# Decay and beta columns taken along by the spatial gate's value projection

## The chip, the cores and the metric

One core of a Trainium2 chip runs the whole program. Its engines work side by side, each through its own list of instructions: TensorE (PE; its weight loads are listed as PEld), VectorE (DVE), ScalarE (ACT), GpSimd (POOL) and SyncE (SP), from whose queue almost all transfers are issued. The metric is device time in microseconds (us) of one execution; lower is better.

## The reference

Two layers of a block whose mixer has four branches of 256 features: a retention, a spatial gate, a short convolution and a gated delta rule. There are 1024 latent and 256 context tokens of 1024 features; all is float32. Per layer, cut to what this change concerns:

```python
h  = rms_norm(x, g_pre[l]) * (1.0 + scale[:, None]) + shift[:, None]       # the same for ctx
p  = h @ w_in[l]                       # 15 pieces of 256 columns, then 4 of 4: a_f, a_b, b_f, b_b
# spatial gate: u, v, z are pieces 4, 5, 6
v = layer_norm_plain(gelu(v));  s = einsum('hij,bnjhd->bnihd', w_s, v) + b_s
y = gelu(u) * s * silu(z)
# gated delta rule: for both directions, chunks of 64 tokens, 4 heads
g    = -exp(a_log) * softplus(a + dt_bias);   beta = sigmoid(b)
gc   = cumsum of g within a chunk;            g_last = its last value
decay = exp(gc_i - gc_j);  k_tail = kc * exp(g_last - gc);  c_dec = exp(g_last)
```

The 16 last columns of `p` give the decays `a` and the betas `b` of 2 directions and 4 heads. The second layer computes outputs for the latent tokens alone, but its keys, values, decays and betas also for the context.

## The kernel before

**Number format.** TensorE multiplies float32 with several passes; the kernel writes both operands of its large products as a high and a low float32r part and adds three products (high x high, high x low, low x high). `halve` makes the parts: ACT casts the high one, POOL (or DVE) subtracts the low one. `H` holds the parts of h, feature-major in three token blocks of 512, 512 and 256.

**Projections.** `projs` (lines 511 to 513) is feature-major: 128 columns of weights are stationary, tokens move, 512 at a time, eight pieces of features one after the other. `proj_tm` (lines 534 to 536) is token-major: 128 tokens of h are stationary and 256 columns of weights move, so a tile of tokens has 24 passes. It serves the values of the spatial gate and of the retention. Both write to one of two PSUM banks of pool `pj`. Weights come through the tags `raw`, `whi` and `wlo`, two buffers each.

**Decays and betas.** They have a product of their own in plain float32: `gate_part` (line 409) multiplies each of the eight pieces of h with 32 columns (16 of them zero) into the bank `pb`, four pieces side by side; `gate_rows` copies `pb` to SBUF on ACT (line 414) and adds the four with a matrix of ones (line 419) into `ab`: rows 32 g + (direction, head), 320 tokens a row. In layer 0 that is done as h is made (`first_h`), in layer 1 within the output stage of layer 0 (`make_h_gates`). `gates` (lines 867 to 918) then makes softplus, betas and the running sums by two scans over the rows, all on [128, 320] tiles on DVE and ACT, stores them to DRAM (`gc`, `last`) and turns them to token-major columns `vtok` by 40 matmuls with selecting matrices (lines 912, 913).

**Order of a layer.** `run` first drains `delta_qkv(l, ctx, 0)`: keys and values of the first pair of heads, then queries; `gates` stands in it behind keys and values. Then for each pair `delta_chain`: triangles, their inverse (`lanes`, `invert`) and 20 steps in a row, three small products each (lines 1107, 1116, 1130) with DVE work between; and `delta_out` (line 1171). What TensorE does in the meantime comes from `fillers`, a generator over short convolution, spatial gate, the second pair's projections (`qkv`), the first pair's gate (`fin0`), and the retention (`rv`, `r0`, `r1`), the other half of the convolution (`sc1`) and `fin1`. `beside(pe, wait)` pulls as much of it as the waits ahead are planned to last; `fin0` gives nothing until the first pair's outputs are there:

```python
self.lead = min(self.lead, 4.0) + pe - wait * 1.4
least = 0.6 * pe
while self.lead < 0 or least > 0:
    us = next(self.flow, None)
```

**The scheduler.** The framework orders each engine's instructions at build time: what is written earlier goes first, and what is written later moves up where an earlier instruction is not ready, as far as tiles can be had. Most tiles are slots of 1280 floats: 10 in pool G, 7 in pool F. In the start-up, loads are chained in order by `inorder`; `ahead` holds the three steps that make h, popped as a projection reaches a token block.

Of the kernel before, what the change touches and what calls it, by code (L numbers as in the profile page):

```python
# [19 lines left out]
P = 128  # L20
D = 1024
KC = 8
# [12 lines left out]
# columns of the constant array  # L35
C_ID = 0
C_SUM = C_ID + 128
C_MASK = C_SUM + 32
# [5 lines left out]
C_ROW = C_INDQ + 32  # L44
C_SELA = C_ROW + 6
C_SELD = C_SELA + 4 * 24
C_PM = C_SELD + 4 * 24
C_PH = C_PM + 2
C_N = C_PH + 2


def constants():
    """Tables that depend on shapes alone."""
# [3 lines left out]
    c[:, C_SUM:C_SUM + 32] = np.tile(np.eye(32), (4, 1))  # L57
# [17 lines left out]
    c[:, C_ROW + 0] = np.where(r < 8, 1.0, np.where(r < 16, -1.0, 0.0))  # L75
    c[:, C_ROW + 1] = np.where(r < 16, -1.0, 0.0)
    c[:, C_ROW + 2] = r < 4
    c[:, C_ROW + 3] = (r >= 4) & (r < 8)
    c[:, C_ROW + 4] = (r >= 8) & (r < 16)
    for g in range(4):  # L80
        for k in range(8):
            a, b = 32 * g + k, 32 * g + 8 + k
            o = C_SELA + g * 24
            c[a, o + k] = 1.0
            c[b, o + 8 + k] = 1.0
            c[b, o + 16 + k] = 1.0
            c[a, C_SELD + g * 24 + 8 + k] = 1.0
    c[:, C_PM] = np.where(r < 16, -1.0, 0.0)
    c[:, C_PM + 1] = np.where(r >= 16, -1.0, 0.0)
    c[:, C_PH:C_PH + 2] = -c[:, C_PM:C_PM + 2]  # L90
    return c


def rotary():
    """cos and signed sin of the grid positions, [d of two heads, (cos | sin), token]."""
# [9 lines left out]
class Block:  # L105
    """The two layers, on one core."""
# [23 lines left out]
    # ---------------------------------------------------------------- tiles  # L130
# [16 lines left out]
    def small(self, shape, nm, bufs=None):  # L147
        self.uid += 1
        k = {} if bufs is None else {"bufs": bufs}
        tag = nm if nm in ("hf", "hg", "wab0", "wab1", "xn") else f"{nm}{self.layer}"  # L150
# [12 lines left out]
    # ---------------------------------------------------------------- set-up  # L163
    def setup(self):
# [33 lines left out]
    def features(self):  # L198
        """Per-feature vectors as columns: the steps that load them, and the one that turns them."""
# [79 lines left out]
    def gate(self, l):  # L279
        """gate * g_post as rows, to DRAM: the steps that make them."""  # L280
# [25 lines left out]
    # ---------------------------------------------------------------- h  # L306
# [5 lines left out]
    def rstd(self, out, ss):  # L312
        """(mean + eps) ** -0.5 of sums over the features"""
# [13 lines left out]
    def first_h(self):  # L327
        """h of the first layer, from the inputs."""
# [40 lines left out]
        def block(b, t0, n):  # L369
# [8 lines left out]
            pb = self.ps("pb")  # L378
            hs = []
            for kc in range(KC):  # L380
# [10 lines left out]
                hs.append(hf)  # L391
                if kc % 4 == 3:
                    for j in range(kc - 3, kc + 1):
                        self.gate_part(pb[:, :n], j, hs[j])
            self.gate_rows(pb, t0, n)

        self.gate_weights(0)
# [3 lines left out]
    def gate_weights(self, l):  # L401
        self.wab = self.small([P, KC, 32], f"wab{l}", 1)
        self.nc.gpsimd.memset(self.wab, 0.0)
        self.inorder(self.nc.sync.dma_start(self.wab[:, :, :16], self.wcols(l, 15 * 256, 16)))
        self.pab = self.ps("ab")

    def gate_part(self, out, kc, h):
        r = 32 * (kc % 4)
        return self.nc.tensor.matmul(out[r:r + 32], lhsT=self.wab[:, kc], rhs=h, start=(kc < 4), stop=(kc >= 4))  # L409

    def gate_rows(self, pb, t0, n):
        """Their sums: rows 32 g + (direction, head), 320 tokens of group g."""
        part = self.small([P, 512], "hg", 1)
        self.nc.scalar.copy(part[:, :n], pb[:, :n])
        t = t0
        while t < t0 + n:
            g, o = t // 320, t % 320
            m = min(320 - o, t0 + n - t)
# [1068 lines left out]
```

## Time and profile before

| | us |
|---|---|
| median of 3 runs (lowest to highest) | 1568.75 (1561.75 to 3282.81) |
| span of the profiled execution | 1566.5 |
| PE busy in it | 1464.3 (93%) |
| DVE, ACT, POOL busy | 815.3, 491.6, 389.0 |

The profile is of one execution, from its first to its last instruction; the median of the runs is 2.25 us above its span. Times in the views count from the span's start. Layer 0 goes to about 872 us (from 738 with its output stage), layer 1 from there on. A busy PE includes the tail of a matmul that the next one overlaps. PE's idle time is mostly in the start-up, in the two inversions of the second pairs and behind the last chain.

### The profile page before, as it was taken

What the parts mean: (1) busy time and instruction counts of PE and PEld (TensorE: products, weight loads), DVE (VectorE), ACT (ScalarE), POOL (GpSimd) and SP (SyncE); (2) the same over time, 40 slices, a digit from 0 to 9 for tenths busy, and PEclk for the clock granted to TensorE, in tenths of its full rate; (3) what the DMA queues carried; (4) which work ended last, traced back from release to release, by engine and by line L of the source; (5) the groups of instructions that cost most, each with busy time, mean ns of one, the idle gap of its engine ahead of it and who ended that gap; (6) DMA issues with size and microseconds to landing.
All of it is one profiled execution on the core that took longest, in us unless ns stands there. A gap on an engine that the chain in (4) does not pass through costs nothing.

```text
span 1566.5 us, 35585 instructions
## 1 busy us (share of the span) xinstructions
PE 1464.3 (93%) x14962; PEld 1133.4 (72%) x14962; DVE 815.3 (52%) x1851; ACT 491.6 (31%) x1053; POOL 389.0 (25%) x567
## 2 busy tenths in 40 slices
PE   4899999999998889999999999999999869999698
PEld 1377887666786666778899787866678557666698
DVE  0656753453277566454355566534543876554333
ACT  3534223212331222324455451322222312322331
POOL 2322222231131113223212132222321312133221
PEclk9899999999999899999999999999999898999899
DMA  8412430235565211036433235322125341113552
GB/s 274 150 28 67 120 68 23 65 126 171 156 157 130 51 50 42 26 116 188 155 122 123 67 78 133 85 69 83 61 72 132 86 102 44 28 55 106 173 193 81
DMA packets 210250, 158.91 MB, mean 101 GB/s; under 512 B 95142, under 2 KB 182442, under 8 KB 210090
## 3 DMA queue, kind: packets, MB, share of 16 engines
q1 hardware_dynamic: 209578, 156.63, 35.8%
q8 instruction: 117, 1.92, 0.5%
q14 instruction: 43, 0.35, 0.1%
q0 software_dynamic: 512, 0.00, 0.0%
HBM read 123.84 MB, written 32.76 MB: 100 GB/s over the span
## 4 chain that ended last, share of the span: by engine, by line
PE 75%; DVE 11%; issue 6%; DMA 4%; ACT 2%; SPq 1%; POOL 1%; DVEq 0%; POOLq 0%; ACTq 0%
PE pj L511 14%; PE pj L513 13%; PE pj L512 12%; PE po L1383 4%; PE po L1381 4%; PE po L1382 4%; PE cb L1116 3%; DVE lt L1227 2%; PE pb L409 2%; PE cb L1130 2%; PE cb L1107 2%; DMA wm<-in_w_mod 1%; DVE xl L1229 1%; POOL wlo L472 1%; PE pt L535 1%
## 5 line engine op out<-in xcount | busy, mean ns | idle before, releaser
L472 POOL TENSOR_TENSOR wlo<-raw,whi 128x512 fp32r<-128x512 f32 x152 | 208.4, 1384 | 593.9 <-ACT whi L471 547.4
L1381 PE MATMUL po<-wo,whi 128*128 128x256 f32 x576 | 163.1, 284 | 1.3 <-ACT wo L471 1.3
L1383 PE MATMUL po<-wo,wlo 128*128 128x256 f32 x576 | 162.7, 282 | 1.2 <-POOL wlo L472 1.2
L1382 PE MATMUL po<-wo,whi 128*128 128x256 f32 x576 | 161.8, 281 | 0.3 <-DVE wo L472 0.3
L1139 POOL COPY gS<-cS 64x64 f32<-64x64 f32 x304 | 86.2, 284 | 284.8 <-DVE cS L1136 261.5
L471 ACT CAST whi<-raw 128x512 fp32r<-128x512 f32 x152 | 92.1, 618 | 179.3 <-PE pj L512 95.4
L1381 PEld LDWEIGHTS po<-wo,whi 128*128 128x128 f32 x576 | 108.8, 189 | 4.4 <-issue 2.4
L1383 PEld LDWEIGHTS po<-wo,wlo 128*128 128x128 f32 x576 | 109.0, 189 | 3.1 <-POOL wlo L472 1.8
L1382 PEld LDWEIGHTS po<-wo,whi 128*128 128x128 f32 x576 | 109.1, 189 | 0.9 <-DVE wo L472 0.5
L1110 DVE SCALAR_TENSOR_TENSOR cy<-cb,vtok,gvt 64x64 f32<-64x64 f32 x304 | 73.8, 280 | 67.5 <-PE cb L1107 66.0
L1124 ACT COPY gx<-cb 64x128 f32<-64x128 f32 x160 | 41.6, 260 | 213.7 <-DVE cw L1121 200.1
L511 PE MATMUL pj<-h10h,whi 128*128 128x512 f32 x200 | 86.7, 434 | 1.8 <-ACT rk L738 1.8
L511 PE MATMUL pj<-h00h,whi 128*128 128x512 f32 x200 | 84.8, 425 | 2.0 <-ACT h00h L385 2.0
L511 PE MATMUL pj<-h11h,whi 128*128 128x512 f32 x200 | 85.2, 426 | 0.0
L511 PE MATMUL pj<-h01h,whi 128*128 128x512 f32 x200 | 83.6, 418 | 0.9 <-ACT gp L928 0.9
L513 PE MATMUL pj<-h00h,wlo 128*128 128x512 f32 x200 | 82.8, 414 | 0.9 <-POOL wlo L472 0.9
L513 PE MATMUL pj<-h10h,wlo 128*128 128x512 f32 x200 | 82.6, 413 | 0.4 <-POOL wlo L472 0.4
L512 PE MATMUL pj<-h10l,whi 128*128 128x512 f32 x200 | 82.4, 412 | 0.0
L512 PE MATMUL pj<-h00l,whi 128*128 128x512 f32 x200 | 82.3, 412 | 0.0
L512 PE MATMUL pj<-h11l,whi 128*128 128x512 f32 x200 | 81.7, 408 | 0.0
L1121 DVE TENSOR_TENSOR cw<-cb,gwt 64x128 f32<-64x128 f32 x152 | 43.9, 289 | 72.6 <-PE cb L1116 70.6
L513 PE MATMUL pj<-h11h,wlo 128*128 128x512 f32 x200 | 80.8, 404 | 0.0
(375 smaller groups left out, 3448.2 us busy)
## 6 DMA issues: line engine op xcount, KB each, us to landing
raw<-in_w_in SPq DMA_DIRECT2D x120, 256.0 KB
wm<-in_w_mod SPq DMA_DIRECT2D x32, 512.0 KB
x<-in_x SPq DMA_DIRECT2D x16, 512.0 KB
wg<-in_w_mod SPq DMA_DIRECT2D x16, 512.0 KB
raw<-yd SPq DMA_DIRECT2D x32, 256.0 KB
gD<-gc SPq DMA_DIRECT2D x32, 160.0 KB
nd<-gN SPq DMA_DIRECT2D x16, 320.0 KB
xd<-x SPq DMA_DIRECT2D x9, 512.0 KB
```

Of the source, the lines that this page charges most:

```text
L471: self.nc.scalar.copy(hi, raw)
L472: (engine or self.nc.gpsimd).tensor_tensor(lo, raw, hi.bitcast(F32), ALU.subtract)
L511: nc.tensor.matmul(b[:, :n], lhsT=hi[:, kc], rhs=hh[:, kc], start=(kc == 0), stop=False)
L512: nc.tensor.matmul(b[:, :n], lhsT=hi[:, kc], rhs=hl[:, kc], start=False, stop=False)
L513: nc.tensor.matmul(b[:, :n], lhsT=lo[:, kc], rhs=hh[:, kc], start=False, stop=(kc == KC - 1))
L1110: done = V.scalar_tensor_tensor(y[rows(c), half(h)], pk[h][rows(c)], vt[rows(c), 3, d, c // 2, h:h + 1], x[d][:, half(h)], ALU.mult, ALU.add)
L1116: last = self.after(nc.tensor.matmul(px[d][rows(c), half(h)], lhsT=Z[d][rows(c), h, c // 2], rhs=x[d][:, half(h)], start=True, stop=True), ...
L1121: done = V.tensor_tensor(heads(xw[rows(c)]), heads(px[d][rows(c)]), wt[rows(c), d, c // 2].unsqueeze(2).to_broadcast([64, 2, 64]), ALU.mult)
L1139: nc.gpsimd.tensor_copy(state(c)[half(d), half(h)], new[half(h), half(d)])
L1381: nc.tensor.matmul(b, lhsT=yh[:, kc], rhs=self.W[0, kc, j], start=kc == 0 and jj == 0, stop=False, skip_group_check=True)
L1382: nc.tensor.matmul(b, lhsT=yh[:, kc], rhs=self.W[1, kc, j], start=False, stop=False, skip_group_check=True)
L1383: held = nc.tensor.matmul(b, lhsT=yl[:, kc], rhs=self.W[0, kc, j], start=False, stop=kc == KC - 1 and jj == 1, skip_group_check=True)
```

## The change

`gate_part`, `gate_rows`, `gate_weights`, `make_h_gates` and their tiles are gone. A new `spatial_v` runs at the head of each layer, ahead of keys and values: it is the spatial gate's value projection, taken out of `spatial`, with the 16 columns of decays and betas behind the 256. In layer 1 the two context tiles get only the 16 columns. `gates` then works on token-major columns, [128 tokens, 10 tiles, 16]; sums within chunks are four matmuls with constant matrices, and one transpose gives the rows for DRAM. The chunk's last sums come to all partitions by two of the four, so that `last` needs no trip through DRAM. Comments and docstrings go as well. The core of the diff:

```diff
 # setup
-        gv = cp.tile([P, DEPTH, 2], F32, name="gv")
-        nc.gpsimd.memset(gv, 0.0)
-        for g in range(4):
-            for j, key in enumerate(("gdn_dt_bias", "gdn_a_log")):
-                for l in range(DEPTH):
-                    nc.gpsimd.dma_start(gv[32 * g:32 * g + 8, l, j:j + 1], a[key][l].rearrange("d (h o) -> (d h) o", o=1))
-        self.gv = gv
+        self.gv = cp.tile([P, 2, DEPTH, 8], F32, name="gv")
+        for j, key in enumerate(("gdn_dt_bias", "gdn_a_log")):
+            nc.sync.dma_start(self.gv[:, j], a[key].rearrange("l d h -> l (d h)").unsqueeze(0).to_broadcast([P, DEPTH, 8]))
...
 # proj_tm
+        n = 272 if gates else 256
...
+            for i in range(2):
+                raw = self.raw([P, 2, n])
+                k = slice(4 * j + 2 * i, 4 * j + 2 * i + 2)
+                self.inorder(nc.sync.dma_start(raw[:, :, :256], self.wcols(l, c0, 256)[:, k]))
+                if gates:
+                    self.inorder(nc.sync.dma_start(raw[:, :, 256:], self.wcols(l, c1, 16)[:, k]))
+                self.halve(hi[:, 2 * i:2 * i + 2], lo[:, 2 * i:2 * i + 2], raw)
...
+        for t in range(NT if gates else len(tiles)):
+            if t % 4 == 0 and self.ahead:
+                self.ahead.pop(0)()
...
+            cols = slice(0, n) if t in tiles else slice(256, n)
+            b = self.bank("pt")[:, cols]
...
+            if t in tiles:
+                evac(b[:, :256], t)
+            if gates:
+                nc.vector.tensor_copy(self.ab[:, t], b[:, -16:])
...
+    def spatial_v(self, l, ctx):
+        nc = self.nc
+        nt = NT if ctx else 8
+        v = [self.slot("sv") for _ in range(2)]
+        st = self.small([P, NT, 6], "sgst", 1)
+        mv = self.small([P, NT, 2], "sgmv", 1)
+        self.ab = self.small([P, NT, 16], "gab", 1)
+
+        def ev_v(b, t):
+            d = v[t // 5][:, 256 * (t % 5):256 * (t % 5) + 256]
+            nc.scalar.activation(d, b, AF.Gelu_apprx_tanh)
+            nc.vector.bn_stats(st[:, t], d)
+            self.have_mv = nc.vector.bn_aggr(mv[:, t], st[:, t])
+
+        yield from self.proj_tm(l, 5 * 256, range(nt), ev_v, True)
+        self.sv = v, mv
...
 # gates
+        g = w[:, 800:880].rearrange("p (t k) -> p t k", k=8)
+        V.scalar_tensor_tensor(g, x3[:, :, :8], -1.0, na.unsqueeze(1).to_broadcast([P, NT, 8]), ALU.mult, ALU.mult)
+        pv = self.ps("vt")
+        for d in range(2):
+            nc.tensor.matmul(pv[:, 40 * d:40 * d + 40], lhsT=cst[:, C_TRI + 128 * d:C_TRI + 128 * d + 128], rhs=g[:, :, 4 * d:4 * d + 4],
+                             start=True, stop=True)
+            nc.tensor.matmul(pv[:, 80 + 80 * d:160 + 80 * d], lhsT=cst[:, C_ALL + 128 * d:C_ALL + 128 * d + 128], rhs=g,
+                             start=True, stop=True)
...
+        self.ec = self.small([P, 2, NT, 8], "gec", 1)
+        nc.scalar.activation(self.ec.rearrange("p q t k -> p (q t k)"), pv[:, 80:240], AF.Exp)
+        pt = self.ps("gcT")
+        nc.tensor.transpose(pt[:80, :P], w[:, 880:960], self.ident)
...
-        for j, src in enumerate((R, eg)):
-            for g in range(4):
-                nc.sync.dma_start(self.gcd[j][:, N * g:N * g + N], src[32 * g:32 * g + 8, :])
-        self.lastd = self.dp.tile([8, 20], F32, name=f"last{self.uid}")
-        for g in range(4):
-            nc.sync.dma_start(self.lastd[:, 5 * g:5 * g + 5], last[32 * g:32 * g + 8, :])
+        for j, src in enumerate((gr, ge)):
+            nc.sync.dma_start(self.gcd[j].rearrange("k (t i) -> (k t) i", i=P), src)
...
 # delta_chain
-        for d in range(2):
-            for h in range(2):
-                i = 4 * d + 2 * hp + h
-                nc.sync.dma_start(ec[64 * h:64 * h + 64, d], self.lastd[i:i + 1, :].to_broadcast([64, 20]))
...
 # output
-            self.gate_weights(l + 1)
...
-                    if hf == 0 and parts is not None:
-                        self.make_h_gates(l + 1, *parts, held)
...
 # run
+            self.flow = self.spatial_v(l, ctx)
+            self.drain()
             self.flow = self.delta_qkv(l, ctx, 0)
             self.drain()
...
-    nc = bacc.Bacc("TRN2", target_bir_lowering=False, num_devices=1)
+    nc = bacc.Bacc("TRN2", target_bir_lowering=False, num_devices=1, dynamic_dma_scratch_size=2048)
```

The constants lose the summing, row and selecting matrices and gain `C_TRI` and `C_ALL`, two 128 x 128 matrices each.

## Rows read from the trace of the kernel before

**Rows 1.** The page, part 1: busy us, share of the span, instructions.

```profile
PE 1464.3 (93%) x14962; PEld 1133.4 (72%) x14962; DVE 815.3 (52%) x1851; ACT 491.6 (31%) x1053; POOL 389.0 (25%) x567
```

**Rows 2.** PE's timeline in the front: start us, length, line, operation, idle before.

```profile
54.51 1.04 PE L409 MATMUL pb<-xT,wab 128*32 128x512 f32 x2
55.48 0.50 PE L513 MATMUL pj<-h00h,wlo 128*128 128x512 f32 x1
...
63.16 0.73 PE L419 MATMUL ab<-hg,cst 128*32 128x320 f32 x4
```

**Rows 3.** Groups by line and shape, both layers: busy us, mean ns, idle.

```profile
L409 PE MATMUL pb<-xn,wab 128*32 128x128 f32 x160 | 13.4, 281 | 0.0
...
L409 PE MATMUL pb<-xT,wab 128*32 128x512 f32 x16 | 9.9, 704 | 0.0
...
L409 PE MATMUL pb<-hb,wab 128*32 128x512 f32 x16 | 6.6, 604 | 0.2 <-ACT hb L388 0.2
...
L409 PE MATMUL pb<-hb,wab 128*32 128x256 f32 x16 | 4.2, 391 | 0.3 <-ACT hb L388 0.3
```

**Rows 4.** PE's timeline in layer 1: first and last of twenty such rows.

```profile
909.90 0.31 PE L912 MATMUL vt<-cst,ga 128*64 128x24 f32 x4
...
912.14 0.30 PE L913 MATMUL vt<-cst,ga 128*64 128x24 f32 x4
```

**Rows 5.** PE's waits, whole span: us in total, times, longest.

```profile
PE vt L912 <- DVE ga L891: 3.9, 1, 3.9
...
PE pt L535 <- POOL wlo L472: 2.0, 3, 0.8
```

**Rows 6.** SP's timeline of transfer issues in the start-up.

```profile
35.25 0.43 SPq L404 DMA_DIRECT2D wab<-in_w_in  x1
```

**Rows 7.** Timelines of PE and PEld in the front.

```profile
66.01 0.39 PE L511 MATMUL pj<-h00h,whi 128*128 128x512 f32 x1
66.24 0.40 PE L512 MATMUL pj<-h00l,whi 128*128 128x512 f32 x1
...
92.31 1.02 PEld L349 LDWEIGHTS xT<-cst,x 128*128 128x128 f32 x8
...
102.06 0.28 PE L512 MATMUL pj<-h02l,whi 128*128 128x256 f32 x1
...
102.18 0.28 PE L513 MATMUL pj<-h02h,wlo 128*128 128x256 f32 x1
```

**Rows 8.** Timelines of DVE and ACT in the front of layer 0.

```profile
56.59 0.69 DVE L390 TENSOR_TENSOR h00l<-xT,h00h 128x512 fp32r<-128x512 f32 x1
...
61.90 0.59 ACT L414 COPY hg<-pb 128x512 f32<-128x512 f32 x1 [7.45 <-PE pb L409]
```

**Rows 9.** PE's timeline at the end of layer 0's first chain.

```profile
371.47 0.44 PE L1116 MATMUL cb<-cy,gZ 64*64 64x64 f32 x4
...
398.59 0.34 PE L1171 MATMUL oi<-gqd,gS 128*64 128x64 f32 x4
```

**Rows 10.** PE's timeline in layer 1: end of the first chain, in the second.

```profile
1156.60 0.39 PE L534 MATMUL pt<-whi,h10h 128*128 128x256 f32 x1
...
1162.72 0.46 PE L1116 MATMUL cb<-cy,gZ 64*64 64x64 f32 x8
...
1167.38 0.44 PE L1116 MATMUL cb<-cy,gZ 64*64 64x64 f32 x4
...
1415.60 0.45 PE L1116 MATMUL cb<-cy,gZ 64*64 64x64 f32 x8
...
1421.32 0.45 PE L1116 MATMUL cb<-cy,gZ 64*64 64x64 f32 x8
```

**Rows 11.** Windows: us, busy of PE, PEld, DVE, ACT, POOL; clock, DMA, GB/s.

```profile
44.00:68.00 24.00, 23.71 (x68) 10.06 (x69) 14.98 (x17) 14.45 (x26) 9.73 (x7) 0.89 0.59 198
...
1168.00:1198.00 30.00, 30.00 (x352) 28.76 (x352) 5.61 (x5) 6.94 (x16) 2.50 (x2) 1.00 0.62 154
...
1240.00:1324.00 84.00, 68.72 (x1324) 52.35 (x1324) 57.48 (x148) 18.45 (x38) 10.61 (x13) 0.83 0.34 79
```

More of the change, by code (lines that the diff above doesn't have):

```diff
@@ L90, in constants @@
     c[:, C_PH:C_PH + 2] = -c[:, C_PM:C_PM + 2]
+    same = p[:, None] // 64 == p[None, :] // 64
+    c[:, C_TRI:C_TRI + 128] = same & (p[:, None] <= p[None, :])
+    c[:, C_TRI + 128:C_TRI + 256] = same & (p[:, None] >= p[None, :])
+    for q in range(2):
+        c[64 * q:64 * q + 64, C_ALL + 128 * q:C_ALL + 128 * q + 128] = 1.0
     return c
@@ L149, in small @@
         k = {} if bufs is None else {"bufs": bufs}
-        tag = nm if nm in ("hf", "hg", "wab0", "wab1", "xn") else f"{nm}{self.layer}"
+        tag = nm if nm in ("hf", "hg", "xn") else f"{nm}{self.layer}"
         return self.mp.tile(shape, F32, tag=tag, name=f"{nm}_{self.uid}", **k)
@@ L390, in block @@
                 (nc.gpsimd if kc % 3 == 2 else nc.vector).tensor_tensor(lo[:, kc], hf, hi[:, kc].bitcast(F32), ALU.subtract)
[L391 to L397, printed above, removed]
-        self.ahead = [lambda b=b, t0=t0, n=n: block(b, t0, n) for b, (t0, n) in enumerate(BLOCKS[True])]
[L401 to L418, printed above, removed]
-            self.nc.tensor.matmul(self.pab[32 * g:32 * g + 32, o:o + m], lhsT=self.cst[:, C_SUM:C_SUM + 32],
-                                  rhs=part[:, t - t0:t - t0 + m], start=True, stop=True)
-            t += m
+        self.ahead = [lambda b=b, t0=t0, n=n: block(b, t0, n) for b, (t0, n) in enumerate(BLOCKS[True])]
     def make_h(self, l, t, x, held):
@@ L452, in make_h @@
             nc.vector.tensor_tensor(lo[dst], h4, hi[dst].bitcast(F32), ALU.subtract)
-        return t, xn
-    def make_h_gates(self, l, t, h, held):
-        off = (t % 4) * P
-        if off == 0:
-            self.pb = self.ps("pb")
-        for kc in range(KC):
-            self.after(self.gate_part(self.pb[:, off:off + P], kc, h[:, kc * P:kc * P + P]), held)
-        if off == 384 or t == NT - 1:
-            self.gate_rows(self.pb, t * P - off, off + P)
     def halves(self, hi, lo, raw, src, engine=None):
@@ L520, in projs, with proj_tm @@
                 yield 6 * n / 2400
-    def proj_tm(self, l, c0, tiles, evac):
+    def proj_tm(self, l, c0, tiles, evac, gates=False):
         nc = self.nc
-        src = self.wcols(l, c0, 256)
-        w = [self.split(src[:, 4 * j:4 * j + 4], [P, 4, 256]) for j in range(2)]
-        for t in tiles:
+        c1 = 15 * 256
+        n = 272 if gates else 256
+        w = []
+        for j in range(2):
+            self.uid += 1
+            hi = self.wp.tile([P, 4, n], F32R, tag="whi", name=f"whi{self.uid}")
+            lo = self.wp.tile([P, 4, n], F32R, tag="wlo", name=f"wlo{self.uid}")
+            for i in range(2):
[5 more added lines that the diff above has]
+                self.halve(hi[:, 2 * i:2 * i + 2], lo[:, 2 * i:2 * i + 2], raw)
+            w.append((hi, lo))
+        for t in range(NT if gates else len(tiles)):
+            if t % 4 == 0 and self.ahead:
+                self.ahead.pop(0)()
             hh, hl = self.H[t // 4]
             o = (t % 4) * P
-            b = self.bank("pt")[:, :256]
+            cols = slice(0, n) if t in tiles else slice(256, n)
+            b = self.bank("pt")[:, cols]
             for kc in range(KC):
-                hi, lo = (x[:, kc % 4] for x in w[kc // 4])
+                hi, lo = (x[:, kc % 4, cols] for x in w[kc // 4])
                 ah, al = hh[:, kc, o:o + P], hl[:, kc, o:o + P]
@@ L616, in spatial @@
             nc.sync.dma_start(bs[q:q + 64, h // 2], a["sg_b"][l, h:h + 1, :].to_broadcast([64, P]))
-        v = [self.slot("sv") for _ in range(2)]
-        st = self.small([P, NT, 6], "sgst", 1)
-        mv = self.small([P, NT, 2], "sgmv", 1)
-        def ev_v(b, t):
-            d = v[t // 5][:, 256 * (t % 5):256 * (t % 5) + 256]
-            nc.scalar.activation(d, b, AF.Gelu_apprx_tanh)
-            nc.vector.bn_stats(st[:, t], d)
-            self.have_mv = nc.vector.bn_aggr(mv[:, t], st[:, t])
-        yield from self.proj_tm(l, 5 * 256, range(nt), ev_v)
         self.rsqrt(mv[:, :nt, 1], mv[:, :nt, 1], self.eps, self.have_mv)
@@ L897, in gates @@
[L897 to L898 removed]
+        self.after(nc.scalar.activation(na, self.gv[:, 1, l], AF.Exp), have_e)
+        g = w[:, 800:880].rearrange("p (t k) -> p t k", k=8)
[6 more added lines that the diff above has]
+                             start=True, stop=True)
@@ new lines, in gates @@
+        vt = self.small([P, NT, 32], "vtok", 1)
+        gk = w[:, 880:960].rearrange("p (k t) -> p k t", t=NT)
+        for d in range(2):
+            p = pv[:, 40 * d:40 * d + 40].rearrange("p (t h) -> p t h", h=4)
+            V.tensor_copy(vt[:, :, 4 * d:4 * d + 4], p)
+            nc.scalar.copy(gk[:, 4 * d:4 * d + 4].rearrange("p h t -> p t h"), p)
+        V.tensor_scalar(vt[:, :, 16:24], x3[:, :, 8:], -1.0, None, ALU.mult)
+        for q in range(2):
+            r = slice(64 * q, 64 * q + 64)
+            V.tensor_tensor(vt[r, :, 8:16], pv[r, 80 + 80 * q:160 + 80 * q].rearrange("p (t k) -> p t k", k=8), vt[r, :, 0:8], ALU.subtract)
@@ L905, in gates @@
-        for g in range(4):
-            nc.sync.dma_start(self.lastd[:, 5 * g:5 * g + 5], last[32 * g:32 * g + 8, :])
-        pv = self.ps("vt")
-        with self.tc.manual_schedule(engines={PE}):
-            for c in range(20):
-                g, o = c // 5, (c % 5) * 64
-                out = pv[64 * (c % 2):64 * (c % 2) + 64, 24 * (c // 2):24 * (c // 2) + 24]
-                nc.tensor.matmul(out, lhsT=R[:, o:o + 64], rhs=cst[:, C_SELA + 24 * g:C_SELA + 24 * g + 24], start=True, stop=False)
-                nc.tensor.matmul(out, lhsT=D1[:, o:o + 64], rhs=cst[:, C_SELD + 24 * g:C_SELD + 24 * g + 24], start=False, stop=True)
```

103 lines of the change are left out of this document (34 added, 69 removed).

## The prediction

> **What bounds the kernel now.** I read the page's busy shares first: TensorE is busy 93% of the span, no other engine over 52% [rows 1], and the chain that ended last runs mostly on PE too. The kernel is bound by the sum of TensorE's work, so I ask of every edit how much PE time goes or comes, and where PE would then stand idle. For that I read the stretches by window and the listing of waits.
>
> The records overlap: a matmul's busy time holds a tail that the next one covers, so I price from start to start. Two 32-column records (one matmul) start 0.97 us before the next product, though 1.04 us busy [rows 2]: 0.93 of the busy column.
>
> **What goes.** In layer 0 the pb products are busy 9.9 + 6.6 + 4.2 = 20.7 us, in layer 1 13.4 us [rows 3]; times 0.93 that is 19.3 and 12.5 us. Their sums into `ab` come three times a layer, 0.73, 0.73 and 0.62 us long of which 0.1 overlaps ([rows 2] has the first): 1.9 us a layer. The 40 selecting matmuls into `vt` stand from 909.90 to 912.44 us, 80 records in 2.5 us [rows 4]; 2.5 us a layer. In layer 0 PE also waits 3.9 us there for the decay chain on DVE [rows 5]; the new sums are ready before the key projection even starts, so I count that wait as gone. Together 27.6 us in layer 0 and 16.9 us in layer 1. On SP 18 small transfers a layer (six of the decay rows, twelve of `last`) and the load of `wab` go; no row shows PE waiting for one, so they count nothing. Four 16-column loads a layer come in ahead of the keys' weights, and two loads of `gv` come to SP in place of sixteen on POOL. At the 0.43 us that a small issue takes on SP [rows 6] that is 1.7 us, hidden by the making of h, and 0.9 us, hidden by PE's wait for `w_mod`, which is all lost if that load is late by as much.
>
> **What comes.** A pass of 256 columns starts every 0.12 us and one of 512 every 0.23 us [rows 7], so 0.45 ns a column; 16 more columns cost 7 ns on 240 matmuls (1.7 us) and 192 (1.4 us). In layer 1 two tiles need only the 16 columns: 48 matmuls, each with a full weight load. No row shows that shape; the nearest are the 128x128 loads, 8 in 1.02 us [rows 7], 0.128 each, and from below the 24-column records, 0.031 each [rows 4]. The weights are the nearer, so I take 0.1: 4.8 us (1.5 to 6.1). The four chunk sums and the transpose are 10 records of at most 0.128: 1.3 us a layer. The wide `whi`, `wlo` pieces of the value projection are held to its last tile, so the key weights are halved only then; with nothing else ready that is a bubble. Rows of such a change show 2.0 us over three waits [rows 5]; 1.5 us a layer (0 to 3).
>
> **The front of layer 0.** Token-major work needs all eight feature pieces of h before its first tile ends, where the old feature-major work took them as they came. The last piece is made at 57.3 us [rows 8], and with two banks only two tiles can run along; two more follow. Against that, ACT's copy of `pb`, which held up the squares of the next tiles for 7.45 us [rows 8], is gone. The new `ab` copies queue on DVE between the pieces of h and release the banks. I charge 4 us (0 to 10). Gelu's table switches are in it.
>
> **Where the moved projection leaves a hole.** The 240 matmuls (29 us in layer 0, 23.6 us for 192 in layer 1) are not new; they move from beside the delta rule to ahead of it. `beside` pulls fillers by a sum that I worked out from the code: in layer 0 the first pair pulls 158.6 of 182.3 planned us up to the end of its chain, and the remaining 23.7 are drained or pulled before the first outputs are done. The chain ends at 371.5 and the output products start at 398.6 [rows 9]. Without the 25.6 us of the value projection, just this drain disappears and the second pair meets the same fillers as before: no loss. In layer 1 the flow gives 153.0 and the chain wants about as much, so 20.5 fewer means none for its last seven steps. There the scheduler moves later ready work up: at 1156.6 us it already put the retention's value projection into the chain's gaps. So filled, a step takes 4.66 us (1162.72 to 1167.38), against 5.72 with pulled fillers [rows 10]; seven steps win 7.4 us. But that projection is then missing after the chain, in a stretch that is 30.0 of 30.0 us busy [rows 11], and the next one needs a slot of the F pool that the gates of the first pair still hold. Between nothing lost and all 23.6 us lost I charge 10, as roughly 18 us of that stretch is the retention's values and 7 are won back.
>
> **The sum.** Layer 0: -27.6 + 1.7 + 1.3 + 1.5 + 4 = -19.1. Layer 1: -16.9 + 1.4 + 4.8 + 1.3 + 1.5 + 10 = +2.1. Together -17.0 us on the span of 1566.5: 1549.5. The median of the runs shown, 1568.75, is 2.25 above the profiled span, so about **1552 us**, 1.1% less. About 2% is what a measurement of this kernel can tell from no change; in these terms I forecast no difference.
>
> **Rivals.**
> *No cover is lost* (0.22). The scheduler finds work for every gap, h keeps up. For it: the mixed steps of a chain are short and hold filler [rows 10], so moving up works. Against: the invert stretch of layer 1 has PE idle for 15 of 84 us with the same scheduler [rows 11]. Without the 10 and the 4, and with the small tiles at their lower end: -17.0 - 14 - 3.3 = -34, or 1535 us.
> *The delta rule starts later and nothing fills it* (0.10, the slower side). Place: the end of the first pair in both layers. It decides if the F pool is full there, since `sv` now holds two of seven slots from the start. Then layer 1 loses 23.6 instead of 10, the front 10 instead of 4, and in layer 0 the wait behind the chain, now covered by the drain (27 us between the two starts [rows 9]), shows for about 15: -17 + 13.6 + 6 + 15 = +17.6, or 1586 us.
> *The clock stays low in the front* (0.08). [...]
> *272 columns do not run at the rate of 256* (0.03): the change would not ride along. At a second pass of 0.12 us on 432 matmuls, +50 us: 1602.
> The forecast itself has 0.57, its own range 1540 to 1566.
>
> **Range and chances.** Left out at most 2 in 10: the slower rival, the 272 columns and half of the first rival's far side. 1530 to 1578. Faster by over 2% is below 1537.4: most of the first rival (0.16) and the forecast's edge (0.06), 0.22. Slower by over 2% is above 1600.1: 0.05. Within: 0.73.
>
> **What would show it.** pb, ab and the old vt records gone, PE's busy sum about 28 us lower; no wait of `vt` for `ga`; the kv projection of layer 0 ending near 117 us in place of 106; the gap between the first pair's chain and its outputs in layer 0 shrinking by about 20 us; in layer 1 the retention's values starting some 20 us before the chain's end, and PE idle behind it. The prediction is wrong if PE stays dense behind that chain (faster), or if the shifted fillers change the idle of an inversion, such as the 15 us of layer 1, by more than 10 us either way.

## The result: 1.5% slower, and the profile after

The changed kernel takes **1588.95 us** in the median (1584.87 to 1594.99, four runs) against 1568.05 for the kernel before beside it: ratio **1.0154, interval [1.0116, 1.0193]**. The forecast was 1552, range 1530 to 1578. One of the four runs of the kernel before took 3282.81 us and is not in the ratio. By the 2% bound this is "no difference", as forecast in words; but the interval excludes one, and the sign is the other way, so the words came true by luck.

Part 1 of the page of the changed kernel answers to [rows 1]: the span, then busy us, share and instructions of each engine.

```profile
span 1585.3 us, 34893 instructions
...
PE 1451.0 (92%) x14636; PEld 1152.0 (73%) x14636; DVE 814.6 (51%) x1863; ACT 503.5 (32%) x1061; POOL 387.4 (24%) x560
```

PE has 13.3 us less work and the span is 18.8 us longer, so about 32 us are new holes. The mark of the forecast was 28 us less; of the difference some 5 us are passes of the front at a granted clock of 0.50 (below). The mean granted clock over the span is 0.954, before 0.971. The next view is the list of PE's waits (us in total, times, longest).

```profile
PE gvT L980 <- ACT rk L709: 10.1, 1, 10.1
...
PE iq L1261 <- issue: 6.8, 3, 3.7
PE ip L1233 <- issue: 6.1, 5, 2.4
...
PE gcT L878 <- ACT ga L864: 5.2, 2, 3.2
PE iq L1223 <- issue: 4.9, 3, 3.5
...
PE pt L496 <- POOL h01l L373: 4.2, 1, 4.2
```

The wait of `vt` for `ga` in [rows 5] is gone, as forecast. What is new or longer stands in the fronts (`h01l`, `gcT`), where layer 1 goes from its first pair to its second (`gvT`, not among the waits of before), and in the inversions: the waits that the profile calls issue ("PE waited for nothing that the profile shows") add up to 20.0 us for `iq` and `ip` in this list's long rows, before to 8.9. The windows below answer to [rows 11]: the front; layer 0's second inversion, from the pair's first `gram` product to the first `iq` (in it DVE inverts small triangles); the products of the inversion of layer 1's first pair, with the chain's first step; the old end of its chain (columns as there).

```profile
44.00:68.00 24.00, 19.64 (x116) 17.47 (x116) 19.18 (x33) 20.58 (x33) 8.18 (x5) 0.83 0.62 206
...
447.60:529.50 81.90, 63.47 (x545) 47.26 (x544) 67.81 (x158) 17.67 (x32) 17.32 (x13) 0.85 0.46 108
...
1039.50:1090.60 51.10, 42.09 (x1105) 30.56 (x1104) 12.85 (x23) 9.14 (x22) 7.05 (x12) 0.80 0.29 96
...
1168.00:1198.00 30.00, 30.00 (x265) 23.98 (x264) 14.45 (x47) 5.36 (x18) 5.94 (x28) 1.00 0.05 15
```

Of the kernel before, the two stretches that answer to the second and the third:

```profile
453.00:525.90 72.90, 61.96 (x500) 45.15 (x500) 59.61 (x147) 14.54 (x26) 17.71 (x13) 0.91 0.53 135
...
1018.90:1055.50 36.60, 33.70 (x1085) 25.55 (x1084) 12.16 (x22) 11.03 (x24) 8.86 (x12) 0.95 0.21 64
```

The same 24 us of the front hold 4.1 us less PE work. The front and both inversions run at a granted clock of 0.80 to 0.85 (before 0.89, 0.91 and 0.95). In layer 1's inversion the 512-column passes behind a hole of 3.5 us start every 0.43 us and not every 0.23 (last section), so there PE loses more than the hole itself.

I cut every trace at the same instructions: the first transpose of the keys (`gkT`) of either layer's first pair, and the first and last output product of layer 0. This table is worked out from the starts of those records (us):

| stage | before | change | place_l0 | place_l1 | cover_l0 | cover_l1 |
|---|---|---|---|---|---|---|
| layer 0, front | 132.8 | 148.7 | 105.6 | 150.0 | 149.7 | 149.3 |
| layer 0, both pairs | 605.3 | 591.4 | 607.3 | 595.0 | 605.9 | 593.2 |
| layer 0, output | 133.5 | 125.9 | 124.9 | 126.6 | 125.4 | 125.6 |
| layer 1, front | 53.2 | 81.3 | 81.1 | 51.4 | 82.7 | 79.1 |
| layer 1, the rest | 641.7 | 638.0 | 630.5 | 634.8 | 634.8 | 628.4 |

Read the second and the last row first: 28.75 us of projection left the pairs of layer 0, and they became 13.9 us shorter; 23.3 us left layer 1's, and the rest became 3.7 us shorter. Layer 0's front grew by 15.9; layer 1's grew by 28.1, of which the shorter output stage gives back 7.6. The last row is known to a few us only: the same layer 1 took 638.0, 630.5 and 634.8 us in three kernels (change, place_l0, cover_l0). With the projection in place beside the same new gates it took 634.8 (place_l1) and 633.4 us (place_both): by these, taking the 23.3 us out gained nothing.

### The profile page after: what moved, and what is told of

Same layout as the page of the kernel before. It is cut to its first block, busy times and chain, and to the rows that moved or that the text cites. A ratio compares the mean times of both kernels' runs of the same rounds, so it can differ in the third digit from the quotient of the medians.

```text
span 1585.3 us, 34893 instructions
## 1 busy us (share of the span) xinstructions
PE 1451.0 (92%) x14636; PEld 1152.0 (73%) x14636; DVE 814.6 (51%) x1863; ACT 503.5 (32%) x1061; POOL 387.4 (24%) x560
## 5 line engine op out<-in xcount | busy, mean ns | idle before, releaser
L416 POOL TENSOR_TENSOR wlo<-raw,whi 128x512 fp32r<-128x512 f32 (+1 forms) x152 | 211.9, 1406 | 613.4 <-ACT whi L415 509.3
L415 ACT CAST whi<-raw 128x512 fp32r<-128x512 f32 (+1 forms) x152 | 92.8, 619 | 144.7 <-PE pj L456 87.3
L456 PE MATMUL pj<-h11l,whi 128*128 128x512 f32 x200 | 81.9, 409 | 0.0
L456 PE MATMUL pj<-h01l,whi 128*128 128x512 f32 x200 | 81.2, 406 | 0.0
```

The source lines that it names most:

```text
L415: self.nc.scalar.copy(hi, raw)
L416: (engine or self.nc.gpsimd).tensor_tensor(lo, raw, hi.bitcast(F32), ALU.subtract)
L456: nc.tensor.matmul(b[:, :n], lhsT=hi[:, kc], rhs=hl[:, kc], start=False, stop=False)
```

## Experiments

Theory A: the moved work was cover; beside the delta rule it cost little, ahead of it it costs in full. A1 puts that in layer 1, A0 puts the loss in layer 0's front. Ratios are to the kernel before, run on the same chip.

**The move alone**, in the kernel before:

```
+            self.flow = self.spatial_v(l, ctx)   # 256 columns, pb stays
+            self.drain()
             self.flow = self.delta_qkv(l, ctx, 0)
```

> The kernel before with one edit: the 256-column value projection of the spatial gate runs ahead of the keys' projection in both layers, as in the changed kernel. pb, ab and the old decay rows stay, no columns ride. In the changed kernel the listing by line shows pb, ab and vt gone (39.5 us) and 1.6 + 6.5 + 3.9 us added (chunk sums, short tiles, 16 columns), which alone would be 28 us less; it is 20 us more, so about 48 us came from somewhere else. Theory A (the move itself costs those 48, wherever it stands): about 1616 us. Theory B (the move costs only because pb no longer fills the front and the gates changed at the same time): 1575 to 1595.

1600.09 us, ratio 1.0225 [1.0178, 1.0272]: 35 us for moving work that is not new. Less than 48: between the two theories' numbers, so a part of the price comes only with the other edits.

**The columns without the move.** In both layers, in layer 1 alone, in layer 0 alone:

```
+            if place:                    # this layer
+                self.no_gates()          # zeros for the 16 columns
+            else:
                 self.flow = self.spatial_v(l, ctx)
                 self.drain()
...
+        if place: yield from self.spatial_v(l, ctx, False)   # in spatial(), as before
```

> The changed kernel with the value projection back in its old place beside the delta rule, 256 columns wide, in both layers; the 16 columns of decays and betas are left out altogether (zeros take their place), the four chunk sums and the new gates stay. So it has what the change removes and nothing of the move. Theory A (the move is what costs): 1568 - 39.5 + 1.6 = about 1530 us. Theory C (the new gates or the missing pb cost too, because something else is late behind them): 1545 or more.

1531.03 us, ratio 0.9795 [0.9731, 0.986]: theory A's 1530 (by the ratio 2.0% under before, where 1530 is 2.4% under 1568; the interval holds both). The removal of pb, ab and the old rows was priced well; what went wrong is in the move and in the columns, which these kernels leave out together with any wait of the gates for them.

> As the kernel with the projection in place, but in layer 1 alone; layer 0 is the changed kernel's. Theory A1 (the loss is lost cover in layer 1's chains, about 24 us, beside the 8 us of the 16 columns and the short tiles left out): 1589 - 32 = about 1557 us. Theory A0 (the loss is the front of layer 0: waits for h and the low clock): 1589 - 8 = about 1581 us.

1558.56 us, 0.9962 [0.9943, 0.998], as A1 expects.

> As the kernel with the projection in place, but in layer 0 alone; layer 1 is the changed kernel's. Theory A0 (front of layer 0: 7 us of passes at the low clock, 8 us of PE idle between 40 and 100 us, the later gates, 2.4 us of columns): 1589 - 25 = about 1564 us. Theory A1 (layer 1's cover): 1589 - 2.4 - at most 8 = 1579 to 1587 us.

1555.83 us, 0.9937 [0.9918, 0.9957], further than A0 expects. So neither layer alone: each gives back 30 us or somewhat more, of which the columns that are left out are some 8 in layer 1 and 2 in layer 0; by the table it is 27 up to layer 0's output products. A0 and A1 were no rivals; the same thing happens twice.

**Is it cover?** The change, with the value projection computed a second time at its old place, for nothing:

```
+        if l == 1:      # the other kernel: l == 0
+            again = self.slot("again")
...
+            yield from self.proj_tm(l, 5 * 256, range(nt), ev_again)
         self.rsqrt(mv[:, :nt, 1], ...
```

> The changed kernel, and in layer 1 the spatial value projection a second time at its old place beside the delta rule: 192 passes of 256 columns, 23.3 us of TensorE by the kernel before, whose result goes to a tile that nothing reads. Theory A1 (the move took cover, so the chains of layer 1 have holes that this work fills): 0 to 10 us more, 1589 to 1599. Rival (TensorE's sum bounds layer 1, and the loss is in its front): 23 us more, 1612.

1580.79 us, ratio 1.0120 [1.0087, 1.0152], against the change's 1.0154 [1.0116, 1.0193]: 23.3 us of useless matmuls make layer 1 **no slower**. The rival's 1612 is out. Where they go can be seen: window of the inversion of layer 1's first pair, in this kernel; the same stretch of the change and of the kernel before stands above.

```profile
1040.30:1077.40 37.10, 34.80 (x1085) 26.54 (x1084) 12.05 (x22) 11.02 (x24) 8.64 (x12) 0.91 0.13 36
```

51.1 us have become 37.1 (36.6 in the kernel before), with the granted clock at 0.91 in place of 0.80; and the wait of `gvT` for `rk` (10.1 us) is no longer among PE's waits. The second is the firmer of the two: in every kernel with layer 1's projection ahead PE is idle for 10.7 to 11.0 us from the second pair's `gkT` to its `gram`, in every one with work in its old place for under 2 (worked out from the records), while the first pair's time from the first `iq` to the chain varies from 34.4 to 46.4 us among the former (31 to 34 in the latter).

> The same for layer 0 alone: 240 more passes, 28.8 us of TensorE, beside its first pair. My forecast took the layer for bound by the sum, so that taking 25.6 us of planned work out of the place saves all of it: then this costs 29 us, 1618. Theory A0 (only about 16 us came back from the place: 13 behind the first chain, the rest elsewhere): 12 to 20 us more, 1601 to 1609.

1597.93 us, ratio 1.0213 [1.018, 1.0246]: 9 us more than the change by the ratios, 14.5 in the row "both pairs" of the profiled runs, for 28.8 us of work. So layer 0 is not bound by its sum either. The window of its second inversion in this kernel, the stretch that is 447.60 to 529.50 in the change:

```profile
472.20:543.80 71.60, 62.42 (x503) 45.60 (x502) 58.52 (x147) 14.77 (x26) 17.04 (x13) 0.90 0.53 132
```

With the work back, the stretch takes 71.6 us as in the kernel before (72.9), not 81.9. PE's waits within it, first in the changed kernel, then with the work back:

```profile
PE rU L736 <- DVE rvd L731: 6.4, 2, 4.6
PE pj L455 <- DVE gvt L982: 3.8, 1, 3.8
PE rU L736 <- ACT hf L728: 3.6, 1, 3.6
PE ro L794 <- DVE rqd L783: 1.8, 1, 1.8
```

```profile
PE rU L743 <- DVE rvd L738: 8.1, 2, 5.1
PE iq L1230 <- DVE xc L1217: 1.1, 1, 1.1
```

The wait of `rU` for `rvd` is in both, and in the kernel before (7.9 us); the others are new in the change. Groups of PE in the same stretch, first of the change, then with the work back:

```profile
L455 PE MATMUL pj<-h01h,whi 128*128 128x512 f32 x16 | 6.8, 425 | 0.5 <-DVE gN L1013 0.5
...
L794 PE MATMUL ro<-rqd,rS 64*64 64x128 f32 x32 | 2.2, 274 | 2.0 <-DVE rqd L783 1.8 <-DVE rS L755 0.2
```

```profile
L455 PE MATMUL pj<-h01h,whi 128*128 128x512 f32 x24 | 9.5, 396 | 0.0
```

In the change the fillers are one projection further on: passes of a projection are missing, and more of the retention's small products (`ro`, none with the work back), each behind a step on DVE or ACT, come where DVE is busy with the inversion.

**The slots.** The kernel before, with the two F slots of `sv` taken from the start:

```
+            self.sv = [self.slot("sv") for _ in range(2)]
+            for v in self.sv:
+                nc.gpsimd.memset(v[:, T - 2:], 0.0)
             self.flow = self.delta_qkv(l, ctx, 0)
```

> The kernel before, in which the two F slots of the spatial values are taken ahead of the first pair's projections in both layers (a small memset writes them), as the changed kernel takes them; no work is moved. My slower rival said that the hole behind the chains decides by the F pool, since sv holds two of its seven slots from the start. Rival's mechanism (slots): layer 1 loses at least half of the 20 us that came back missing there, layer 0 half of 15: 1575 to 1585, ratio 1.010 or more. Theory A (the work itself is missing as cover, slots are not): ratio 0.997 to 1.004.

1570.85 us, ratio 1.0052 [1.0023, 1.0081], between the two. The trace splits it: layer 1 is not later (691.6 us from layer 0's last output product to the end, before 694.9); layer 0 is 5.5 us later, all of it ahead of its first pair's chain, not behind it. So holding these two slots does not by itself make the hole in layer 1. The hole does end with a slot of that pool, though; rows of the changed kernel:

```profile
1236.37 1.29 DVE L821 TENSOR_TENSOR go<-go,gz 128x512 f32<-128x512 f32 x2
1237.69 1.07 ACT L709 COPY rk<-pj 128x512 f32<-128x512 f32 x2 [9.59 <-DVE go L821]
1238.82 1.97 PE L980 MATMUL gvT<-cst,gp 128*128 128x128 f32 x8 [10.11 <-ACT rk L709]
```

ACT's copy of the retention's keys `rk` waits for the last reading of `gz`, of the first pair's gate; by the code both are slots of pool F. DVE had waited 9.48 us there for `gf`, the gate's norms, to come back from DRAM.

**The front of layer 0.** PE's wait of 4.2 us is for a subtract on POOL. Here are POOL and DVE of the changed kernel in that stretch (start, length, instruction):

```profile
70.94 6.97 POOL L373 TENSOR_TENSOR h01l<-hb,h01h 128x512 fp32r<-128x512 f32 x2 [14.56 <-DVE h01h L372]
```

```profile
72.05 1.28 DVE L373 TENSOR_TENSOR h01l<-hb,h01h 128x512 fp32r<-128x512 f32 x2
73.26 1.09 DVE L372 CAST h01h<-hb 128x512 fp32r<-128x512 f32 x3
74.26 1.28 DVE L373 TENSOR_TENSOR h01l<-hb,h01h 128x512 fp32r<-128x512 f32 x2
```

Of the two on POOL one took 5.72 us and the other, which began after DVE had stopped, 1.29; one on DVE takes 0.68. Edit:

```
-  (nc.gpsimd if kc % 3 == 2 else nc.vector)
+  (nc.gpsimd if kc % 3 == 2 and b == 0 else nc.vector)
```

> The changed kernel with every low part of h in blocks 1 and 2 subtracted on DVE, none on POOL. In the changed kernel PE waits 4.2 us at 76.7 us for such a subtract on POOL, two of which take 7.0 us, and starts again at the low clock. Theory F: 4 to 7 us less, 1582 to 1585. Rival (DVE is as late with them): 1587 to 1592.

1577.08 us, ratio 1.0096 [1.0071, 1.0121], 0.6% under the change's (the two intervals just meet). More than expected; 7.6 us of it are in layer 0 by the stages (740.1 to 732.5 us up to the first output product). PE and the clock between 66 and 80 us, in the changed kernel and in this one:

```profile
66.00:80.00 14.00, 8.21 (x52) 7.33 (x51) 8.34 (x20) 8.48 (x13) 6.97 (x2) 0.88 0.00 1
```

```profile
66.00:80.00 14.00, 12.29 (x95) 11.62 (x96) 11.86 (x34) 11.11 (x19) 0.00 (x0) 1.00 0.01 2
```

The same edit in the kernel before:

> The control of the run with the subtracts on DVE: the kernel before with the same edit, every low part of h in blocks 1 and 2 on DVE. There PE waits for no such subtract on POOL. Theory F (the stall on POOL is of the changed front): within 3 us of before, 1560 to 1567. Rival (the edit is worth 12 us to any front): 1552.

1566.3 us, ratio 1.0032 [1.0015, 1.005]: in the kernel before the edit gains nothing, it even costs a little. The stall belongs to the new order.

Next, the order turned round:

```
             yield from kv
+            yield from self.spatial_v(l, ctx)      # and not ahead of it
             self.gates(l)
```

> The changed kernel with the order of the two projections ahead of the delta rule turned round in both layers: keys and values first (feature-major, 512 columns a pass), then the spatial value projection with the 16 columns, then the gates. Theory F (in layer 0's front the token-major work waits for all of h, about 11 us of idle and 7 us of low clock): layer 0 wins 10 to 15 us, layer 1 nothing, 1573 to 1580. Rival (the gates, now late by the 30 us of the other projection, are covered by the queries' 15 us only): 1590 to 1610. Either way the lost cover beside the chains stays, so it does not come near 1565.

1580.15 us, ratio 1.0114 [1.0083, 1.0144], at the slow end of theory F's 1573 to 1580: layer 0's front is 10.4 us shorter (138.3), but 6.8 of them come back at the first products of the pair, where the late gates now show.

Then both edits together:

> The changed kernel with both edits to the front that helped by themselves: keys and values first, and the subtracts of blocks 1 and 2 on DVE. If they take away the same wait for h (block 1's): as with the subtracts alone, ratio to before 1.007 to 1.010, about 1575. If they take away different waits: about 1566. In neither case below before, since the cover of layer 1 (about 22 us) is still missing.

1579.15 us, ratio 1.0104 [1.0082, 1.0126]: as the subtracts alone. The two repairs take away the same wait, that for block 1 of h.

And the normalization held back:

```
-        self.rsqrt(mv[:, :nt, 1], mv[:, :nt, 1], self.eps, self.have_mv)
+        self.rsqrt(mv[:, :nt, 1], mv[:, :nt, 1], self.eps, self.have_eg)
```

> The changed kernel with the normalization of the spatial values (its logarithm, exponential and ten tensor_scalars) held behind the gates' last exponential. In the changed kernel it stands ahead of the gates on DVE (102.8 to 109.6 us) and brings table loads on ACT. Theory G (late gates cost time in the fronts): 3 to 8 us a layer less, 1573 to 1583. Rival (the keys' and values' projection covers the gates, so their delay is free): 1586 to 1592.

1586.67 us, ratio 1.0163 [1.012, 1.0205]: nothing. My theory G falls; the front became 2.3 us shorter and the rest did not follow.

**The columns in another way**, with no move:

```
+        for kc in range(KC):     # 32 columns: 16 high, 16 low
+            nc.tensor.matmul(pb[:32, :n], lhsT=self.wg[:, kc], rhs=hh[:, kc], ...)
+            nc.tensor.matmul(pb[:16, :n], lhsT=self.wg[:, kc, :16], rhs=hl[:, kc], ...)
```

> Another way to the same columns, with no move: the value projection stays beside the delta rule as in the kernel before; decays and betas come feature-major beside the keys' projection, from one stationary tile that holds the 16 high and the 16 low columns side by side: 16 passes a block in place of 24, paced as 512 columns, 0.23 us. Ten small selecting products a layer make them token-major; the four chunk sums are the changed kernel's. By the kernel with the projection in place in both layers (1531), plus two layers of 16 x (0.23 + 0.23 + 0.12) = 9.3 us and about 2 us of selecting: theory A (only the move cost) 1554. Rival (the fronts become late through the extra copies and the gates): 1562 or more.

1576.52 us, ratio 1.0088 [1.0064, 1.0111]. Theory A missed by 22 us: the kernel it was worked out from had no gates that wait for columns. PE's waits in its front:

```profile
PE pj L489 <- POOL h01l L375: 4.5, 1, 4.5
PE vt L887 <- DVE ga L883: 3.0, 1, 3.0
```

With a block's columns ahead of its keys and the subtracts on DVE:

> The feature-major way to the columns, with the products of a block ahead of its keys, the last block's ahead of the values of the block before, and the subtracts of blocks 1 and 2 on DVE. In the run before this one the gates of both layers were late (PE waited 3.0 us for each, and the keys' transposes came 20 us and 18 us later than with the gates' columns left out, where 11 were new work). If the late gates and the subtract on POOL are the difference: 1576 - 2 x 6 - 8 = about 1556, below the kernel before. If the extra copies on ACT and DVE are: 1570 or more.

1561.72 us, ratio 0.9984 [0.9959, 1.0009]. Both waits are shorter or gone (layer 0's front 121.8 us, 126.9 in the run above); layer 1's front is 63.9 against 53.2.

With layer 1's first two blocks in the output stage of layer 0:

> The feature-major columns of the last such run for layer 0; for layer 1 the products of its first two blocks go into the output stage of layer 0, where the kernel before has its pb products, and only the last block's beside the keys' projection. The value projections stay in place in both layers. From the listing by stretch: layer 0's front is 11 us shorter than before, layer 1's front was 10.6 us longer and the output stage 7.5 us shorter. With most of the columns back in the output stage: front of layer 1 within 3 us of before, output stage 2 to 5 us shorter: 11 + 3 = 14 us under before, ratio 0.990. Rival (the columns cost the same wherever they stand, or the gates of layer 1 are late all the same): 0.997 to 1.000.

1563.43 us, ratio 1.0001 [0.9981, 1.0021]: the rival. The columns cost about 10 us a layer wherever they stand (output stage 135.9 here, 126.0 in the run before). Better than the change by 1.5%, but no version beat the kernel before.

**The short tiles.** Of the change:

```
-            cols = slice(0, n) if t in tiles else slice(256, n)
+            cols = slice(0, n)
```

> The changed kernel with the two tiles of layer 1 that need only the 16 columns computed at the full 272. In the changed kernel their 48 passes start every 0.11 us at first and every 0.21 us at the end, and the granted clock is 0.63 in their last 3.5 us and 0.50 in the next 3.5, though PE has no gap. Theory: passes of 16 columns let the clock fall; then the 48 passes take 6.1 us at 0.127 in place of 6.5, the clock stays 1.00, and the keys' first passes start every 0.23 us: 2 to 3 us less up to the keys' end. Rival (the clock falls for another reason there, such as the waits before): the clock falls all the same, and nothing is won.

One run, 1583.2 us; what counts is the stretch. First the changed kernel, around the end of its 48 passes of 16 columns (895.0 to 901.5 us) and the keys' first passes; then this one:

```profile
895.00:898.00 3.00, 3.00 (x30) 3.00 (x29) 0.81 (x4) 2.79 (x5) 0.43 (x1) 1.00 0.00 0
898.00:901.50 3.50, 3.50 (x23) 3.50 (x22) 0.00 (x0) 0.43 (x3) 2.07 (x2) 0.63 0.31 80
901.50:905.00 3.50, 3.50 (x9) 2.78 (x10) 3.32 (x5) 1.24 (x2) 2.42 (x2) 0.50 0.29 73
```

```profile
895.00:898.00 3.00, 3.00 (x26) 3.00 (x26) 0.65 (x3) 0.39 (x1) 0.00 (x0) 1.00 0.00 0
898.00:901.50 3.50, 3.50 (x30) 3.50 (x29) 1.24 (x5) 2.87 (x6) 0.10 (x1) 1.00 0.00 0
901.50:905.00 3.50, 3.50 (x28) 3.42 (x27) 3.50 (x7) 0.34 (x1) 2.58 (x2) 1.00 0.26 71
```

With 17 times the columns in those passes the clock stays at 1.00, and layer 1's front is 2.9 us shorter. The theory holds.

## Why the prediction was wrong, step by step

The forecast put the span 17.0 us down, it went 18.8 up: 35.8 us to account for.

**What goes: right.** pb, ab and vt fell by 30.7, 3.7 and 5.1 us from start to start, 39.5 in all; the steps had 40.6 for the matmuls alone. That the wait for `ga` goes was right; 5.2 us of `gcT` waiting for `ga` came in its place (two waits). The place_both run agrees with the whole item (2.0% [1.4, 2.7] less).

**What comes: slightly under.** 272 columns start every 0.127 us, 256 every 0.118: 9 ns on 432 passes, 3.9 us (forecast 3.1). The rival "272 columns do not run at the rate of 256" is out. Chunk sums and `gcT` took 1.7 us (2.6). Waits for weights on POOL (`wlo`) stayed as small as forecast: 1.0 us in layer 0's front, 0.7 in layer 1's. The 48 short passes took 6.5 us (4.8), and the keys' first passes behind them start every 0.43 us, at a granted clock of 0.50, where wide_tiles has 0.23 at 1.00: some 2 more.

**The front of layer 0: 6.3 us short.** By the steps it would grow by 28.75 + 1.7 + 1.3 + 1.5 + 4 - 27.6 = 9.6; it grew by 15.9, and the keys' and values' projection ends near 126 us and not 117. The "4 (0 to 10)" for h was the mis-sized term: PE waits 4.2 us for `h01l` on POOL, and 38 of 240 passes run at a granted clock of 0.50 (up to 52.3 us and from 76.7 to 79.6), 10.0 us where 4.8 would do at the 0.127 above. That is the rival "the clock stays low in the front" in part: 5.2 us, and not all of it new, since in the kernel before this stretch starts at 0.50 too (44 to 48 us). From 48.2 to 49.1 us, and from 77.8 to 79.4 us, behind the hole at 72.2 to 76.7, a pass of 272 columns starts every 0.23 us; from 80.0 us on, at 1.00, every 0.13.

**The output stage and front of layer 1: 5.1 us short** (20.5 us more from layer 0's first output product to `gkT`, forecast 15.4): short tiles, their clock, `gcT`'s wait.

**"Where the moved projection leaves a hole": the step that failed.** The text had two parts. *Layer 0: "just this drain disappears and the second pair meets the same fillers as before: no loss."* The drain did shrink: the 27.1 us of [rows 9] became 11.7, as PE's timeline of the changed kernel shows:

```profile
394.27 0.44 PE L1082 MATMUL cb<-cy,gZ 64*64 64x64 f32 x4
...
405.96 0.34 PE L1137 MATMUL oi<-gqd,gS 128*64 128x64 f32 x4
```

 But the fillers met by the second pair were not the same: its inversion (first product of the second `gram` to the first `iq`, 72.9 to 81.9 us) has PE idle 18.4 us against 10.9, at a clock of 0.85 for 0.91. Up to the chain's first product it is 27.8 against 16.9 us idle; over both pairs 34.5 against 24.1, so all the new idle time stands there, and the rest, some 4 us, goes with the lower clock there. Of 28.75 us moved, 13.9 came back: 14.9 lost where the step had 0. *Layer 1: 10 us of 23.3 lost.* By the table it was 19.6, beside the same gates all of it; cover_l1 shows that by putting the work back at no cost. So the first premise fell too: this stretch is not bound by the sum of TensorE's work. The retention's values did move up, as in [rows 10]: they begin at 1155.81 us, 40 us ahead of the chain's end and not 20. And PE is dense behind the chain, where I looked for the hole; it stands further on, as 10.1 us of `gvT`, and ahead, in the inversion. The reason that the text gave, a slot of the F pool that the first pair's gates still hold, is what the rows of `rk` show; its place and its size were wrong.

```profile
1155.43 0.44 PE L1082 MATMUL cb<-cy,gZ 64*64 64x64 f32 x4
1155.81 0.38 PE L494 MATMUL pt<-whi,h10h 128*128 128x256 f32 x1
...
1196.67 0.44 PE L1082 MATMUL cb<-cy,gZ 64*64 64x64 f32 x4
```

 Together 34.5 for 10: 24.5 of the 35.8 us. The remaining 11.4 are the two fronts.

**Why the replay of the fillers misled.** It counted how much work `beside` hands out, in TensorE us. It did not ask which filler comes at which place. Shifted by one projection, retention steps that hang on DVE land in an inversion that keeps DVE at 67.8 of 81.9 us. With the work back DVE is as busy there (58.5 of 71.6), but PE has projections that do not wait for it. My own mark for being wrong (the idle of an inversion changes by more than 10 us) is what happened, just, in layer 0, if its products up to the chain are taken in (10.9); the example that I named for it, the 15 us of layer 1's second pair, changed by some 2 us.

**The slower rival** had 0.10 and 1586 us, with 23.6, 10 and 15 us as its terms; measured are 19.6, 4 + 6.3 and 14.9. Its numbers were right and its mechanism only in part: in layer 1 a full F pool does hold up `rk`, but holding `sv`'s two slots alone costs nothing there, and the 15 us of layer 0 stand in the second pair's inversion, not behind the first chain. It deserved more weight than the forecast. The argument for "no loss" rested on one sum; the argument against stood in my own rows: PE idle for 15 of 84 us in an inversion *with* all fillers in place [rows 11].

**The gaps called issue.** Within runs of 80 small products in layer 1's inversion the change has 9.0 us of them, cover_l1 2.3. No semaphore explains them, but they go with transfers: every such gap ahead of `iq` or `ip`, 14 in the changed kernel and 8 in the kernel before, ends 1.2 to 1.6 us after a 16 KB transfer of the queue that the page lists as instruction has landed. The changed kernel has 115 of these; what they carry was not shown. The two longest gaps, 3.5 and 3.7 us, both have a burst of weight loads right ahead: the transfer (first packets at 1043.74 and 1071.13 us) comes only as the DMA share falls (windows, columns as above):

```profile
1041.80:1043.70 1.90, 0.83 (x73) 0.69 (x73) 0.00 (x0) 0.00 (x0) 0.00 (x0) 1.00 1.05 332
1043.70:1046.10 2.40, 0.00 (x0) 0.00 (x0) 0.00 (x0) 0.00 (x0) 0.00 (x0) 0.91 0.17 40
1068.00:1071.10 3.10, 1.86 (x87) 1.21 (x86) 3.01 (x6) 0.44 (x1) 0.74 (x1) 1.00 1.04 362
1071.10:1073.60 2.50, 0.02 (x4) 0.03 (x4) 0.97 (x2) 0.00 (x0) 0.00 (x0) 0.88 0.13 35
...
q8 instruction: 115, 1.88, 0.5%
```

No run varied these loads or these transfers, so that the burst delays the transfer, and the transfer PE, is the author's reading of the trace, not shown by an experiment.

**Left open.** What layer 1's inversion would take without these gaps is not known. And sub_on_dve gains 9 us by the ratios, of which the stages up to layer 0's outputs show 7.6.

## To carry to other kernels

Work that rides along costs nothing only if its carrier does not move. Before you move a filler out of a latency-bound loop, ask what the same filler would cost there if you added it a second time: if the answer is nothing (as here in layer 1), taking it out gains nothing, and you pay for it in full at its new place. Counting the microseconds of cover isn't enough: look at which filler then falls on which wait, and on which engine that filler itself hangs.

## What was not expected of the hardware

**The clock fell during 48 passes of 16 columns, without a gap.** One started every 0.11 us at first; the granted clock was 1.00 in the first 3.0 us, 0.63 in the last 3.5 and 0.50 in the 3.5 behind them. The same passes at 272 columns, one every 0.127, stayed at 1.00 (both stretches above). PE's busy column is full in both. In place_l0, which has the same short passes, the clock fell too: 1.00 from 867.0 to 870.0 us, 0.60 up to 873.2 and 0.50 up to 877.0.

**Passes behind a hole of 3.5 us took nearly twice as long.** PE's timeline in layer 1's inversion, changed kernel: 512-column passes start every 0.43 us behind the gap, at a granted clock of 0.50, where [rows 7] have 0.23.

```profile
1046.13 0.30 PE L1223 MATMUL iq<-xc,gN 32*32 32x16 f32 x8 [3.50 <-issue]
1046.36 0.80 PE L455 MATMUL pj<-h11h,whi 128*128 128x512 f32 x1
1046.95 0.63 PE L456 MATMUL pj<-h11l,whi 128*128 128x512 f32 x1
1047.38 0.63 PE L457 MATMUL pj<-h11h,wlo 128*128 128x512 f32 x1
1047.81 0.63 PE L455 MATMUL pj<-h11h,whi 128*128 128x512 f32 x1
```

**A subtract on POOL took 5.72 us beside a busy DVE** (busy for 4.6 of them) and 1.29 alone. In the kernel before, the same two took 1.98 and 1.40, with DVE busy for 1.6 and 1.4 us beside them. The long one ended 1.1 us after DVE's last cast or subtract there. So a busy DVE was not enough to make it long, and what was is not shown.
